# A matrix product with rotary embedding on one core: PSUM banks as separate tiles, half-width tiles in the last four pairs, and the first transposes inside the preceding tile

## The chip, the core and the metric

The kernel runs on one core of one Trainium2 chip. The metric is the device time of one execution in microseconds (us). Five engines with queues of their own work side by side: TensorE (PE in the profile) multiplies matrices and writes to PSUM, a memory of eight banks, each of which holds 512 fp32 columns on 128 partitions; VectorE (DVE), ScalarE (ACT) and GpSimd (POOL) do elementwise work; SyncE (SP) issues transfers. Any of SP, ACT and POOL can issue DMA transfers from its queue.

## The reference

```python
batch, seq, hidden, n_heads = (16, 512, 768, 12)      # head_dim = 64
y = np.matmul(x, weight)                              # (16, 512, 768) @ (768, 768), fp32
y = y.reshape(batch, seq, n_heads, head_dim)
y1, y2 = y[..., :32], y[..., 32:]                     # halves of every head
out1 = y1 * cos1 - y2 * sin1                          # cos, sin: (512, 64), cut the same way
out2 = y2 * cos2 + y1 * sin2
out = np.concatenate([out1, out2], axis=-1).reshape(batch, seq, hidden)
```

All of `x` (25 MB) is read and all of `out` (25 MB) is written once.

## The kernel before

**Tiles and pairs.** The 8192 rows of `x` are cut into 64 tiles of 128 rows. Two tiles form a pair; `n` from 0 to 31 counts the pairs (`NP` is 32), `s` is 0 or 1 within a pair, and this text numbers the tiles `i = 2n + s`. A pair's rows share their positions in the sequence, so one set of cos and sin values serves both of its tiles.

**The way of a tile.** SP loads it as fp32 (`xs`, ten buffers). ACT converts it to fp16 (`cast`, recorded at line 74). TensorE transposes it in six 128x128 pieces into a PSUM tile `pt` (`transpose`, line 124, two buffers), and ACT copies that back to SBUF as `xT` (line 74 again). Then TensorE does twelve matmuls (`mm`, line 167): six chunks of the contraction, each over 768 columns that lie in two PSUM banks, so 512 and 256 columns or the reverse. The two tiles of a pair fill one PSUM tile of three banks, of which there are two (`py_pool`). VectorE multiplies each result by cos and by the signed sin at once (`rope`, line 181, with an output `tq` twice as wide), GpSimd adds the two products with the halves of each head exchanged (`add`, line 192, into `ov`), and ACT issues the transfer that stores `ov` (`store`, line 241).

**Block pairs.** Pairs 8, 11, 14, ... 29 (`BLOCKS`) take another way: GpSimd's queue loads them, converted to fp16 on the way (`load_blocks`), and VectorE transposes them (line 131). Neither ACT nor TensorE's transposes take part.

**The order.** The program's order is the order of every engine's queue (`manual_schedule`). `upto("turn", k)` emits transposes until tiles below `k` have them, and `upto("cast", k)` the same for conversions. In the main loop the call after tile `i` is `upto("turn", i + 3)` and `upto("cast", i + 5)`; `upto` adds to `k` an extra lead that grows by one every four tiles from `k = 35` to at most six, so late in the kernel transposes run up to six tiles further ahead. At the start the tiles 0 to 3 are handled by hand around the loading of the weights, and `warm` runs matmuls of zeros until data is there.

**The end.** From pair 28 on (`ALONE = 4`) each tile has two banks of its own. Every third of them takes the two `pt` buffers (named `psz`), since no transpose needs these any more. Each tile is then multiplied, added and stored by itself. The stores of pairs 25, 26 and 27 are emitted at the end of pair 27, on ACT's queue. The last tile (`rope_last`) multiplies its last 256 columns as usual and then does the 512 others on VectorE alone, in three instructions at lines 220 and 224, after which SP stores them.

Of the kernel before, what the change touches and what calls it, by code (L numbers as in the profile page):

```python
# [10 lines left out]
FP32 = mybir.dt.float32  # L11
FP16 = mybir.dt.float16
# [5 lines left out]
def kernel(  # L18
# [9 lines left out]
    nc = tc.nc  # L28
    P = nc.NUM_PARTITIONS

    B, S, H = x.shape
    NH = int(n_heads)
    D = H // NH
    HD = D // 2
    R = 32
    NQ = P // R
    NT = H // (2 * P)
    SB = S // P
    NP = B * SB // 2
    CHUNKS = [(t, e) for t in range(NT) for e in range(2)]  # L40
    AHEAD = 7
    AHEAD_B = 8
    ALONE = 4
# [11 lines left out]
    cold = konst.tile([P, 512], FP16)  # L55
    sin_sb = konst.tile([P, SB, D], FP32)
    csn = konst.tile([P, 2, SB, D], FP32)
    w_raw = konst.tile([P, NT, 2, H], FP32)
    w_sb = konst.tile([P, NT, 2, H], FP16)

    xpool = ctx.enter_context(tc.tile_pool(name="xpool", bufs=10))
    bpool = ctx.enter_context(tc.tile_pool(name="bpool", bufs=5))
    cpool = ctx.enter_context(tc.tile_pool(name="cpool", bufs=6))
    tpool = ctx.enter_context(tc.tile_pool(name="tpool", bufs=11))
    rpool = ctx.enter_context(tc.tile_pool(name="rpool", bufs=3))
    opool = ctx.enter_context(tc.tile_pool(name="opool", bufs=6))
    pt_pool = ctx.enter_context(tc.tile_pool(name="pt", bufs=2, space=bass.MemoryType.PSUM))
    py_pool = ctx.enter_context(tc.tile_pool(name="py", bufs=2, space=bass.MemoryType.PSUM))

    xss, xhs, x16, xTT, psys, tqs, ovs = {}, {}, {}, {}, {}, {}, {}  # L70

# [47 lines left out]

    def transpose(n, s, eng):  # L120
        xc = x16.pop((n, s)).rearrange("p (t m e) -> p t e m", t=NT, e=2)
        pt = pt_pool.tile([P, NT, 2, P], FP16, tag="pt", name="pt")
        for t, e in CHUNKS:
            nc.tensor.transpose(pt[:, t, e, :], xc[:, t, e, :], ident)  # L124
        xT = tpool.tile([P, NT, 2, P], FP16, tag="xT", name="xT")
        copy(eng, xT, pt)
        xTT[n, s] = xT
# [12 lines left out]


    def psum(n, s):
        if n < NP - ALONE:
            if n not in psys:
                psys[n] = py_pool.tile([P, 3, 512], FP32, tag="psy", name="psy")
            cut = 512 if s == 0 else 256
            return [
                (psys[n][:, s, ds(s * 256, cut)], 0, cut),
                (psys[n][:, s + 1, 0 : H - cut], cut, H),
            ]  # L150
        if (n, s) not in psys:
            if (2 * (n - NP + ALONE) + s) % 3 == 1:
                psys[n, s] = [
                    pt_pool.tile([P, 512], FP32, tag="pt", name="psz") for _ in (0, 1)
                ]
            else:
                ps = py_pool.tile([P, 3, 512], FP32, tag="psy", name="psy")
                psys[n, s] = [ps[:, 0], ps[:, 1]]
        lo, hi = psys[n, s]
        return [(lo, 0, 512), (hi[:, 0 : H - 512], 512, H)]  # L160

    def mm(n, s, t, e, c0=0, c1=H):
        for k, (ps, lo, hi) in enumerate(psum(n, s)):
            a, z = max(c0, lo), min(c1, hi)
            if a >= z:
                continue
            nc.tensor.matmul(  # L167
                ps[:, a - lo : z - lo],
                xTT[n, s][:, t, e, :],
                w_sb[:, t, e, a:z],  # L170
                start=((t, e) == CHUNKS[0] and n > 1),
                stop=((t, e) == CHUNKS[-1] and (n > 1 or s >= k)),
            )

    def rope(n, c0, c1, ps):
        r = n % SB
        nh = (c1 - c0) // D
        if n not in tqs:
            tqs[n] = rpool.tile([P, 2, 2 * H], FP32, tag="tq", name="tq")
            ovs[n] = opool.tile([P, 2 * H], FP32, tag="ov", name="ov")  # L180
        nc.vector.tensor_tensor(  # L181
            out=tqs[n][:, :, c0:c1].rearrange("p j (h d) -> p j h d", d=D),
            in0=ps.rearrange("p (h d) -> p h d", d=D)
            .unsqueeze(1).broadcast_to((P, 2, nh, D)),
            in1=csn[:, :, r, :].unsqueeze(2).broadcast_to((P, 2, nh, D)),
            op=MULT,
        )

    def add(n, c0, c1, eng):
        w = c1 - c0  # L190
        tq = tqs[n][:, :, ds(c0, w)]
        eng.tensor_tensor(  # L192
            out=ovs[n][:, ds(c0, w)].rearrange("p (h t d) -> p h t d", t=2, d=HD),
            in0=tq[:, 0].rearrange("p (h t d) -> p h t d", t=2, d=HD),
            in1=tq[:, 1].rearrange("p (h t d) -> p h t d", t=2, d=HD)[:, :, ::-1, :],
            op=ADD,
        )

    def rope_pair(n, step=2 * H):
        ps = psys[n].rearrange("p b n -> p (b n)")  # L200
        for c in range(0, 2 * H, step):
            rope(n, c, c + step, ps[:, ds(c, step)])
            add(n, c, c + step, nc.gpsimd)

    def rope_alone(n, s):
        for ps, lo, hi in psum(n, s):
            rope(n, s * H + lo, s * H + hi, ps)

    def rope_last(n, s):
        (ps, _, cut), (pz, _, _) = psum(n, s)
        c0, c1, c2 = s * H, s * H + cut, (s + 1) * H
        rope(n, c1, c2, pz)
        add(n, c1, c2, nc.gpsimd)
        nh = cut // D
        q = tqs[n][:, 1, c0:c1]
        ph = ps.rearrange("p (h d) -> p h d", d=D)
        for o, j in ((q.rearrange("p (h d) -> p h d", d=D), 1), (ph, 0)):
            nc.vector.tensor_tensor(  # L220
                out=o, in0=ph, op=MULT,
                in1=csn[:, j, n % SB, :].unsqueeze(1).broadcast_to((P, nh, D)),
            )
        nc.vector.tensor_tensor(  # L224
            out=ovs[n][:, c0:c1].rearrange("p (h t d) -> p h t d", t=2, d=HD),
            in0=ps.rearrange("p (h t d) -> p h t d", t=2, d=HD),
            in1=q.rearrange("p (h t d) -> p h t d", t=2, d=HD)[:, :, ::-1, :],
            op=ADD,
        )
        store(n, nc.sync, c0, c1)  # L230
        store(n, nc.scalar, c1, c2)

    def store(n, eng, c0=0, c1=2 * H):
        b, r = where(n, 0)
        dst = out.rearrange("b (p r) h -> r p b h", r=SB)[r, :, b : b + 2]
        src = ovs[n].rearrange("p (b h) -> p b h", b=2)
        if c1 - c0 < 2 * H:
            s = c0 // H
            dst = dst[:, s, c0 - s * H : c1 - s * H]
            src = src[:, s, c0 - s * H : c1 - s * H]  # L240
        eng.dma_start(out=dst, in_=src)


    WARM = 17
    opened = [0]

    def warm(k):
        for _ in range(k):
            n, b = divmod(opened[0] % 6, 3)
            psum(n, 0)  # L250
            nc.tensor.matmul(  # L251
                psys[n][:, b], cold[:, 0:P], cold, start=True, stop=opened[0] < WARM - 6
            )
            opened[0] += 1

# [22 lines left out]
        load_pair(n)  # L278

    done = {"cast": 4, "turn": 4}

    def upto(what, k):
        k += min(6, max(0, k - 31) // 4)
        while done[what] < min(k, 2 * NP):
            n, s = divmod(done[what], 2)
            done[what] += 1
            if what == "cast":
                if n not in BLOCKS:  # L290
                    cast(n, s, nc.scalar)
            elif n in BLOCKS:
                transpose_blocks(n, s)
            else:
                transpose(n, s, nc.scalar)
# [33 lines left out]
    load_blocks(BLOCKS[0], (0, 2))  # L329
    load_blocks(BLOCKS[0], (1, 3))  # L330
    rope_pair(0)
    upto("cast", 6)
    for c in CHUNKS[4:]:
        mm(1, 0, *c)
    for c in CHUNKS[:3]:
# [1 line left out]
    upto("turn", 5)  # L337
    for c in CHUNKS[3:]:
        mm(1, 1, *c)
    upto("cast", 7)  # L340
    upto("turn", 6)
    upto("cast", 8)
    rope_pair(1)

    for n in range(2, NP):
        load_pair(n + AHEAD - 2)
        for m, quarters in ((n + AHEAD_B, (0, 2)), (n + AHEAD_B - 1, (1, 3))):
            if m > BLOCKS[0]:
                load_blocks(m, quarters)
        for s in (0, 1):  # L350
            for c in CHUNKS:
                mm(n, s, *c)
            upto("turn", 2 * n + s + 3)
            upto("cast", 2 * n + s + 5)
            if n >= NP - ALONE:
                if (n, s) != (NP - 1, 1):
                    rope_alone(n, s)
                    add(n, s * H, (s + 1) * H, nc.gpsimd)
                    store(n, nc.scalar, s * H, (s + 1) * H)
        if n < NP - ALONE:  # L360
            if n >= 3:
                store(n - 3, nc.scalar)
            rope_pair(n, H if n >= NP - ALONE - 2 else 2 * H)
        if n == NP - ALONE - 1:
            for m in (n - 2, n - 1, n):
                store(m, nc.scalar)
    rope_last(NP - 1, 1)


# [1 line left out]
_INS = ['x', 'weight', 'cos', 'sin', 'n_heads']  # L371
# [31 lines left out]
```

## Time and profile before

| What | Value |
|---|---|
| median of 8 runs | 158.37 us (158.28 to 158.71) |
| the profiled execution: its own time | 158.32 us |
| its span, first to last instruction | 156.5 us |
| granted TensorE clock, mean | 0.992 |
| busy: PE, DVE, ACT, POOL | 148.4, 124.9, 74.5, 129.1 us |
| DMA | 49.99 MB, mean 319 GB/s |

A line of the timeline gives the start in us, the time from the first start to the last end of the merged instructions, the engine, the line of the kernel, the operation, output and inputs, and how many instructions were merged; brackets hold the idle time before and what ended it. `ACTq`, `SPq` and `POOLq` are the engines' instruction queues, where transfers are issued. A line of the groups gives the shape of an instruction, how often it ran, its busy time in us and the mean duration of one in ns. Matmul records overlap: a matmul's end in the record is modelled, and the distance between two starts is what it costs TensorE.

### The profile page before, as it was taken

Reading aid. Unit: us, or ns where it says so; the run is one execution under the profiler, and the core shown is the slowest. Engines: PE = TensorE matmul, PEld = TensorE weight load, DVE = VectorE, ACT = ScalarE, POOL = GpSimd, SP = SyncE. Lnnn points to the kernel's source line nnn. Section 1 sums busy time; section 2 is a strip of 40 time slices with the busy share of each in tenths; the row PEclk is TensorE's granted clock in tenths of the full one; section 3 lists DMA queues with packets and bytes.
Section 4 is the critical chain, followed back from the end, with each engine's and each line's share of the span. In section 5 each row is a group of like instructions: output and inputs, shape, how many; then the busy total and the mean of one; then the engine's idle time right before and its main releaser. Section 6 shows DMA issues by size and latency. Waiting matters only on the chain.

```text
span 156.5 us, 2722 instructions
## 1 busy us (share of the span) xinstructions
PE 148.4 (95%) x1074; PEld 93.5 (60%) x1074; DVE 124.9 (80%) x78; ACT 74.5 (48%) x93; POOL 129.1 (82%) x77
## 2 busy tenths in 40 slices
PE   6999999999999999999999999999999999999930
PEld 2465666666656656666666666766667666656610
DVE  0656967876698698879869798879697899799990
ACT  3250967766526454660755665674746656200000
POOL 1000599999899899899989989997998779999990
PEclk9999999999999999999999999999999999999996
DMA  4999999999999999999999999999995725499655
GB/s 152 361 412 394 403 365 342 340 403 358 365 362 378 311 397 385 276 402 365 274 383 327 326 302 411 306 379 360 290 372 54 298 104 201 173 392 400 246 203 201
DMA packets 25837, 49.99 MB, mean 319 GB/s; under 512 B 10208, under 2 KB 10720, under 8 KB 25824
## 3 DMA queue, kind: packets, MB, share of 16 engines
q10 hardware_dynamic: 8768, 24.91, 40.9%
q1 hardware_dynamic: 8352, 21.76, 38.0%
q0 software_dynamic: 8704, 3.15, 17.5%
q8 instruction: 8, 0.13, 0.3%
q14 instruction: 5, 0.04, 0.1%
HBM read 27.79 MB, written 25.17 MB: 338 GB/s over the span
## 4 chain that ended last, share of the span: by engine, by line
PE 91%; DVE 4%; POOL 1%; POOLq 0%; issue 0%; DVEq 0%
PE psy L167 75%; PE pt L124 10%; PE psy L251 4%; DVE tq L181 3%; PE psz L167 2%; POOL ov L192 1%; POOLq L398 0%; DVE xT L76 0%; DVE cold L258 0%; DVE w_sb L111 0%; POOLq L192 0%; DVEq L181 0%
## 5 line engine op out<-in xcount | busy, mean ns | idle before, releaser
L167 PE MATMUL psy<-w_sb,xT 128*128 128x256 f16 (+1 forms) x733 | 126.7, 326 | 0.4 <-DVE w_sb L111 0.2
L181 DVE TENSOR_TENSOR tq<-psy,csn 128x3072 f32<-128x3072 f32 (+3 forms) x40 | 102.8, 2591 | 19.7 <-PE psy L167 19.7
L192 POOL TENSOR_TENSOR ov<-tq 128x1536 f32<-128x1536 f32 (+2 forms) x38 | 110.4, 2922 | 7.0 <-DVE tq L181 6.7
L167 PEld LDWEIGHTS <-xT 128*128 128x128 f16 x769 | 73.2, 98 | 45.7 <-DVE xT L131 0.8
L74 ACT COPY xT<-pt 128x768 f16<-128x768 f16 x46 | 36.4, 799 | 52.0 <-PE pt L124 50.5
L74 ACT CAST xc<-xs 128x768 f16<-128x768 f32 x46 | 40.4, 903 | 8.0 <-DMA xs<-in_x_dram 7.9
L124 PEld LDWEIGHTS <-xc 128*128 128x128 f16 x288 | 20.2, 99 | 6.8 <-DVE xc L76 0.9
L124 PE MATMUL pt<-ident,xc 128*128 128x128 f16 x288 | 23.9, 222 | 0.0
L103 POOL DMA_DIRECT2D xh<-in_x_dram x32 | 18.8, 591 | 0.0
L328 POOL COPY mark<-xs 128x1 f32<-128x1 f32 x1 | 0.2, 183 | 16.0 <-DMA xs<-in_x_dram 16.0
L131 DVE STREAM_TRANSPOSE xT<-xh 128x384 f32<-128x384 f32 x16 | 10.6, 690 | 0.0
L251 PE MATMUL psy<-cold 128*128 128x512 f16 x17 | 6.9, 557 | 1.2 <-DVE cold L258 1.2
L167 PE MATMUL psz<-w_sb,xT 128*128 128x512 f16 (+1 forms) x36 | 6.3, 326 | 0.0
L111 DVE CAST w_sb<-w_raw 128x768 f16<-128x768 f32 (+2 forms) x7 | 3.4, 500 | 2.0 <-DMA w_raw<-in_weight_dram 2.0
L76 DVE CAST xc<-xs 128x768 f16<-128x768 f32 x2 | 1.9, 948 | 3.2 <-DMA xs<-in_x_dram 3.2
L181 DVE TENSOR_TENSOR tq<-psz,csn 128x512 f32<-128x512 f32 (+1 forms) x5 | 4.3, 897 | 0.1
L251 PEld LDWEIGHTS <-cold 128*128 128x128 f16 x17 | 2.0, 131 | 3.5 <-issue 2.2
L76 DVE COPY xT<-pt 128x768 f16<-128x768 f16 x2 | 1.1, 558 | 1.6 <-PE pt L124 1.6
L74 ACT ACT_TABLE_LOAD x1 | 1.3, 1283 | 0.7 <-PEq L384 0.7
L258 DVE MEMSET cold<- 128x256 uint32 x1 | 0.3, 272 | 0.9 <-PEq L384 0.9
L224 DVE TENSOR_TENSOR ov<-psz,tq 128x512 f32<-128x512 f32 x1 | 0.7, 692 | 0.0
L220 DVE TENSOR_TENSOR psz<-psz,csn 128x512 f32<-128x512 f32 x1 | 0.7, 690 | 0.0
(9 smaller groups left out, 2.0 us busy)
## 6 DMA issues: line engine op xcount, KB each, us to landing
out_dram<-ov ACTq DMA_DIRECT2D x28, 768.0 KB, 7.2
xs<-in_x_dram SPq DMA_DIRECT2D x48, 384.0 KB, 6.7
xh<-in_x_dram POOLq DMA_DIRECT2D x32, 96.0 KB, 8.1
out_dram<-ov ACTq DMA_DIRECT2D x7, 384.0 KB, 2.4
w_raw<-in_weight_dram SPq DMA_DIRECT2D x5, 384.0 KB, 7.1
w_raw<-in_weight_dram SPq DMA_DIRECT2D x1, 256.0 KB, 5.7
out_dram<-ov SPq DMA_DIRECT2D x1, 256.0 KB, 2.6
w_raw<-in_weight_dram SPq DMA_DIRECT2D x1, 128.0 KB, 5.5
```

The source lines that it names most:

```text
L74: eng.copy(out=o, in_=i_)
L76: eng.tensor_copy(out=o, in_=i_)
L103: nc.gpsimd.dma_start(out=dst[ts(q, R)], in_=src[r, q])
L111: nc.vector.tensor_copy(out=w_sb[:, t, e, c0:c1], in_=w_raw[:, t, e, c0:c1])
L124: nc.tensor.transpose(pt[:, t, e, :], xc[:, t, e, :], ident)
L131: nc.vector.transpose(out=xT.bitcast(FP32).rearrange("p t (j a) o -> p t j (a o)", j=NQ), in_=x16.pop((n, s)).bitcast(FP32).rearrange("p ( ...
L167: nc.tensor.matmul(ps[:, a - lo : z - lo], xTT[n, s][:, t, e, :], w_sb[:, t, e, a:z], start=((t, e) == CHUNKS[0] and n > 1), stop=((t, e) ...
L181: nc.vector.tensor_tensor(out=tqs[n][:, :, c0:c1].rearrange("p j (h d) -> p j h d", d=D), in0=ps.rearrange("p (h d) -> p h d", d=D) .unsqu ...
L192: eng.tensor_tensor(out=ovs[n][:, ds(c0, w)].rearrange("p (h t d) -> p h t d", t=2, d=HD), in0=tq[:, 0].rearrange("p (h t d) -> p h t d", ...
L220: nc.vector.tensor_tensor(out=o, in0=ph, op=MULT, in1=csn[:, j, n % SB, :].unsqueeze(1).broadcast_to((P, nh, D)),)
L224: nc.vector.tensor_tensor(out=ovs[n][:, c0:c1].rearrange("p (h t d) -> p h t d", t=2, d=HD), in0=ps.rearrange("p (h t d) -> p h t d", t=2, ...
L251: nc.tensor.matmul(psys[n][:, b], cold[:, 0:P], cold, start=True, stop=opened[0] < WARM - 6)
```

## The change

PSUM is taken as single banks: `py_pool` has six buffers of one bank in place of two of three, and the multiplication by cos and sin runs bank by bank (`rope_bank`), the first bank of a pair right after the pair's first tile. In the last four pairs a tile is two halves of 384 columns, each in a bank of its own; `mm` runs all six chunks for one half, then for the other, and each half is multiplied and added by itself. Only the last half of the last tile goes through `rope_last`. For pairs 2 and 3 each tile's matmuls are cut at a column (256, or 512 for tile 4), and the transposes of the tile two further on, with the next conversion, stand between the two parts; the conversions of tiles 5 to 10 are emitted later than before. The growing extra lead in `upto` is gone, and `tpool` has 8 buffers in place of 11. In the last four pairs `upto` stands ahead of the tile's matmuls.

```diff
-    tpool = ctx.enter_context(tc.tile_pool(name="tpool", bufs=11))
+    tpool = ctx.enter_context(tc.tile_pool(name="tpool", bufs=8))
-    py_pool = ctx.enter_context(tc.tile_pool(name="py", bufs=2, space=bass.MemoryType.PSUM))
+    py_pool = ctx.enter_context(tc.tile_pool(name="py", bufs=6, space=bass.MemoryType.PSUM))
...
     def psum(n, s):
...
+        key, banks = (n, 3) if n < NP - ALONE else ((n, s), 2)
+        if key not in psys:
+            psys[key] = [
+                py_pool.tile([P, 512], FP32, tag="psy", name="psy") for _ in range(banks)
             ]
+        ps = psys[key]
+        if banks == 2:
+            return [(ps[k][:, 0:HH], k * HH, (k + 1) * HH) for k in (0, 1)]
+        cut = 512 if s == 0 else 256
+        return [(ps[s][:, ds(s * 256, cut)], 0, cut), (ps[s + 1][:, 0 : H - cut], cut, H)]
...
+    def rope_bank(n, b):
+        rope(n, b * 512, (b + 1) * 512, psys[n][b])
+
+    def add_pair(n, step=2 * H):
         for c in range(0, 2 * H, step):
-            rope(n, c, c + step, ps[:, ds(c, step)])
             add(n, c, c + step, nc.gpsimd)
...
+    def rope_pair(n):
+        for b in range(3):
+            rope_bank(n, b)
+        add_pair(n)
...
-    def rope_last(n, s):
-        (ps, _, cut), (pz, _, _) = psum(n, s)
-        c0, c1, c2 = s * H, s * H + cut, (s + 1) * H
-        rope(n, c1, c2, pz)
-        add(n, c1, c2, nc.gpsimd)
-        nh = cut // D
+    def rope_last(n, ps, c0, c1):
+        nh = (c1 - c0) // D
...
-        k += min(6, max(0, k - 31) // 4)
         while done[what] < min(k, 2 * NP):
...
     rope_pair(0)
-    upto("cast", 6)
+    upto("cast", 5)
...
     upto("turn", 5)
     for c in CHUNKS[3:]:
         mm(1, 1, *c)
-    upto("cast", 7)
-    upto("turn", 6)
-    upto("cast", 8)
+    upto("cast", 6)
     rope_pair(1)
...
         for s in (0, 1):
-            for c in CHUNKS:
-                mm(n, s, *c)
-            upto("turn", 2 * n + s + 3)
-            upto("cast", 2 * n + s + 5)
-            if n >= NP - ALONE:
-                if (n, s) != (NP - 1, 1):
-                    rope_alone(n, s)
-                    add(n, s * H, (s + 1) * H, nc.gpsimd)
+            i = 2 * n + s
+            if n < 4:
+                cut = 512 if i == 4 else 256
+                for c0, c1 in ((0, cut), (cut, H)):
+                    for c in CHUNKS:
+                        mm(n, s, *c, c0, c1)
+                    if c0 == 0:
+                        upto("turn", i + 2)
+                        upto("cast", i + 3)
+            elif n < NP - ALONE:
+                for c in CHUNKS:
+                    mm(n, s, *c)
+            upto("turn", i + 3 if i > 6 else 0)
+            upto("cast", i + 5 if i > 6 else 0)
+            if n < NP - ALONE:
+                for b in ((0,), (1, 2))[s]:
+                    rope_bank(n, b)
+                continue
+            for ps, lo, hi in psum(n, s):
+                for c in CHUNKS:
+                    mm(n, s, *c, lo, hi)
+                c0, c1 = s * H + lo, s * H + hi
+                if (n, s, hi) == (NP - 1, 1, H):
+                    rope_last(n, ps, c0, c1)
+                    store(n, nc.sync, c0, c1)
+                    continue
+                rope(n, c0, c1, ps)
+                add(n, c0, c1, nc.gpsimd)
+                if (n, s) == (NP - 1, 1):
+                    store(n, nc.scalar, c0, c1)
+                elif hi == H:
                     store(n, nc.scalar, s * H, (s + 1) * H)
         if n < NP - ALONE:
             if n >= 3:
                 store(n - 3, nc.scalar)
-            rope_pair(n, H if n >= NP - ALONE - 2 else 2 * H)
+            add_pair(n, H if n >= NP - ALONE - 2 else 2 * H)
         if n == NP - ALONE - 1:
             for m in (n - 2, n - 1, n):
                 store(m, nc.scalar)
-    rope_last(NP - 1, 1)
```

More of the change, by code (lines that the diff above doesn't have):

```diff
@@ L37 @@
     NT = H // (2 * P)
+    HH = H // 2
     SB = S // P
@@ L121, in transpose @@
         xc = x16.pop((n, s)).rearrange("p (t m e) -> p t e m", t=NT, e=2)
-        pt = pt_pool.tile([P, NT, 2, P], FP16, tag="pt", name="pt")
+        bank = pt_pool.tile([P, 8, P], FP16, tag="pt", name="pt")
+        pt = bank[:, 0 : 2 * NT].rearrange("p (t e) m -> p t e m", e=2)
         for t, e in CHUNKS:
@@ L142, in psum @@
     def psum(n, s):
[L143 to L149, printed above, removed]
-            ]
[L151 to L160, printed above, removed]
+        key, banks = (n, 3) if n < NP - ALONE else ((n, s), 2)
+        if key not in psys:
+            psys[key] = [
+                py_pool.tile([P, 512], FP32, tag="psy", name="psy") for _ in range(banks)
+            ]
+        ps = psys[key]
[3 more added lines that the diff above has]
+        return [(ps[s][:, ds(s * 256, cut)], 0, cut), (ps[s + 1][:, 0 : H - cut], cut, H)]
     def mm(n, s, t, e, c0=0, c1=H):
@@ L197, in add @@
         )
-    def rope_pair(n, step=2 * H):
-        ps = psys[n].rearrange("p b n -> p (b n)")
+    def rope_bank(n, b):
+        rope(n, b * 512, (b + 1) * 512, psys[n][b])
+    def add_pair(n, step=2 * H):
         for c in range(0, 2 * H, step):
-            rope(n, c, c + step, ps[:, ds(c, step)])
             add(n, c, c + step, nc.gpsimd)
-    def rope_alone(n, s):
-        for ps, lo, hi in psum(n, s):
-            rope(n, s * H + lo, s * H + hi, ps)
-    def rope_last(n, s):
-        (ps, _, cut), (pz, _, _) = psum(n, s)
-        c0, c1, c2 = s * H, s * H + cut, (s + 1) * H
-        rope(n, c1, c2, pz)
-        add(n, c1, c2, nc.gpsimd)
-        nh = cut // D
+    def rope_pair(n):
[4 more added lines that the diff above has]
+        nh = (c1 - c0) // D
         q = tqs[n][:, 1, c0:c1]
@@ L229, in rope_last @@
         )
-        store(n, nc.sync, c0, c1)
-        store(n, nc.scalar, c1, c2)
     def store(n, eng, c0=0, c1=2 * H):
@@ L251, in warm @@
             nc.tensor.matmul(
-                psys[n][:, b], cold[:, 0:P], cold, start=True, stop=opened[0] < WARM - 6
+                psys[n][b], cold[:, 0:P], cold, start=True, stop=opened[0] < WARM - 6
             )
```

## The prediction

> **What bounds the kernel now.** I read the page first: busy time, then the chain that ended last.
>
> ```profile
> span 156.5 us, 2722 instructions
> PE 148.4 (95%) x1074; PEld 93.5 (60%) x1074; DVE 124.9 (80%) x78; ACT 74.5 (48%) x93; POOL 129.1 (82%) x77
> ...
> PE 91%; DVE 4%; POOL 1%; POOLq 0%; issue 0%; DVEq 0%
> ```
>
> The chain is TensorE for 91% of the span: whatever makes TensorE wait lengthens the kernel, and only what shortens its queue, its waits or the tail behind it can gain. In the chain's list a tile's twelve matmuls take 1.95 us and six transposes 0.34 us, 2.29 together, so 512 of a tile's columns cost 1.30 and 256 cost 0.65. Next, the timeline of the start:
>
> ```profile
> 15.35 1.91 ACT L74 CAST xc<-xs 128x768 f16<-128x768 f32 x2 [4.65 <-DMA xs<-in_x_dram]
> ...
> 17.16 0.80 ACT L74 COPY xT<-pt 128x768 f16<-128x768 f16 x1
> ...
> 17.84 0.50 PE L124 MATMUL pt<-ident,xc 128*128 128x128 f16 x6
> 17.85 0.90 ACT L74 CAST xc<-xs 128x768 f16<-128x768 f32 x1
> ...
> 18.52 2.11 PE L167 MATMUL psy<-w_sb,xT 128*128 128x512 f16 x12 [0.18 <-DVE tq L181]
> ...
> 20.47 0.50 PE L124 MATMUL pt<-ident,xc 128*128 128x128 f16 x6
> ...
> 21.00 0.80 ACT L74 COPY xT<-pt 128x768 f16<-128x768 f16 x1 [0.76 <-PE pt L124]
> ```
>
> Two things are to be seen. The transposes from 17.84 are through at 18.18, yet tile 4's matmuls start at 18.52, when the multiplication of all of pair 0 lets its banks go: 0.34 us lost, the largest gap after the start. And the way from a transpose to a usable `xT` is long: transposes through at 20.81, ACT's copy from 21.00 to 21.80. ACT's next instruction starts 0.70 after a copy's start and 0.80 after a conversion's (17.16, 17.85, 18.65); TensorE starts about 0.13 after its operand is written (the conversion that ends at 5.29 is followed by transposes at 5.43). From then on TensorE runs without a break: tile 9 starts at 29.94, tile 56 at 134.21. Last, the end:
>
> ```profile
> 128.77 7.02 POOL L192 TENSOR_TENSOR ov<-tq 128x1536 f32<-128x1536 f32 x3 [1.09 <-DVE tq L181]
> ...
> 133.87 0.50 PE L124 MATMUL pt<-ident,xc 128*128 128x128 f16 x6
> ...
> 134.21 2.11 PE L167 MATMUL psy<-w_sb,xT 128*128 128x512 f16 x12
> 134.41 0.80 ACT L74 COPY xT<-pt 128x768 f16<-128x768 f16 x1 [1.49 <-PE pt L124]
> 134.41 18.66 ACTq L241 DMA_DIRECT2D out_dram<-ov  x12
> 135.98 16.71 POOL L192 TENSOR_TENSOR ov<-tq 128x768 f32<-128x768 f32 x10 [0.19 <-DVE tq L181]
> ...
> 150.62 0.68 DVE L220 TENSOR_TENSOR tq<-psz,csn 128x512 f32<-128x512 f32 x1
> 151.21 0.69 DVE L220 TENSOR_TENSOR psz<-psz,csn 128x512 f32<-128x512 f32 x1
> 151.94 0.69 DVE L224 TENSOR_TENSOR ov<-psz,tq 128x512 f32<-128x512 f32 x1
> 152.66 0.35 SPq L241 DMA_DIRECT2D out_dram<-ov  x1
> ```
>
> ACT's last copy is at 134.41, and all that follows on its queue are stores. Pair 25's sum was ready at about 132.2 (first of the three from 128.77), but its store left only behind that copy: ACT's queue goes in order, stores included. GpSimd then takes 16.71 us for ten sums, and ACT's queue sits in stores that wait for them, with nothing behind them. The last matmuls end at 134.21 + 8 x 1.95 = 149.81; the last store leaves SP at 152.66.
>
> **The start, part by part.** Bank by bank, pair 0's first bank is free after one instruction of 1.22 us (the 128x1024 row) in place of one of 3.36, at about 16.3, and the 0.34 goes. But the later order puts ACT on TensorE's path. Tile 5's conversion now follows tile 4's copy. Tile 4's copy starts at 16.87 + 0.20 = 17.07 (its transposes end at 16.87) and ends at 17.87, tile 4's matmuls start at 18.00 (TensorE was free at 17.84: 0.16 lost). Its 512 columns last to 19.30, tile 5's transposes (converted by 18.67) to 19.63, the other 256 columns to 20.29. Tile 5's copy runs 19.83 to 20.63, so tile 5 starts at 20.76: 0.47 lost. Its first 256 columns end at 21.42; tile 6's conversion, behind the copy, runs 20.53 to 21.43, its transposes start at 21.56: 0.14 lost. With 512 columns behind the transposes (1.30) tiles 6 and 7 come in time. In tile 7 two sets are due: tile 8's transposes end at 26.48, its copy starts at 26.68, the conversion of tile 9 at 27.38, done 28.28, and TensorE, through at 27.78, can transpose tile 9 only at 28.41: 0.63 lost. Tile 9's matmuls start at 31.03 against 29.94. Sum: 0.16 + 0.47 + 0.14 + 0.63 - 0.34 = +1.1 us. Tile 6 is cut into one piece more per chunk, six matmuls, at 0.11 each for 256 columns: the columns are the same, nothing. From tile 9 on the order is the old one.
>
> **The middle.** Three multiplications of 1.22 for one of 3.35 are 0.30 per pair, for pairs 0 to 27 8.4 us more on VectorE. What hides it is VectorE's idle time, 19.7 us behind TensorE in the waits, and each bank's own release, earlier than before; uncovered it would cost those 8.4. I take nothing. ACT's stores of pairs up to 24 find their sums long done. Loads wait for the buffers of tiles converted long before.
>
> **The end.** Without the extra lead, the transposes of tiles 57 and 60 to 63 come later: four sets (4 x 0.34) move from before tile 55's end to behind it. TensorE's sum is the same, but ACT's conversions and copies for tiles 60 to 63 now stand behind stores. Count from X, the end of pair 27's matmuls (before: 133.87; after: 133.87 + 1.1 - 1.34 = 133.6). VectorE starts the second bank at X + 0.27, the third at X + 1.40. GpSimd's two sums of pair 27 (1.82, or 1.77 where they follow closely) run X + 1.53 to X + 5.13, the store of pair 27 leaves at X + 5.16 and holds the queue for 0.38, and only then comes the conversion of tile 60: X + 5.6 to X + 6.5. TensorE had transposes of tile 57, tiles 56 and 57, through at X + 0.34 + 3.90 = X + 4.24; the next thing in its queue is tile 60's transposes, at X + 6.63: 2.4 us lost, with tile 58's matmuls, ready long since, queued behind. By rows the wait is at least 1.6 (the second sum starts as soon as the third bank is multiplied, at X + 2.6) and at most 3.0 (the store's issue takes 1.0, the longest of this line, in place of its 0.38).
>
> Later conversions and copies just come in time: tile 61's (behind the store of tile 56, whose second half is added by X + 7.05) is done at X + 8.4 for X + 8.9; tile 62's at X + 11.0 for X + 11.2; tile 63's at X + 13.2 for X + 13.5. So the matmuls end at X + 6.63 + 4 x 0.335 + 6 x 1.95 = X + 19.7 = 153.3, against 149.81.
>
> **The tail** gets shorter. The first half of the last tile is multiplied by 0.2 after the last matmul; then VectorE's last three instructions are 384 wide. The 512-wide ones take 2.01 from first start to last end; at 1.05 ns per column (681 to 1217 ns from 512 to 1024 elements) 384 wide they take 1.61, between 2.01 (nothing saved) and 1.0 (half). They end at 153.3 + 0.25 + 1.61 = 155.2, SP's store leaves 2.5 later than 152.66. A last transfer of 192 KB in place of 256 and 128 may give 0.1. GpSimd has no arrears after TensorE's stall: the last half's sum ends 1.2 after the matmuls. So 158.32 + 2.5 - 0.1 = 160.7 us; the profiled run was 0.05 below the median.
>
> **A rule on the clock.** The trace shows the clock's price at the start: a 512-column matmul cost 0.43 us (4.45 for ten) and costs 0.216 from 7.4 us on. A gap of 2.4 us on warm hardware is not in this trace; the bounds are no effect and the start's 5.9 us at half speed, which would add 2.95. I take none, the nearest rows being the 0.34 gap, behind which the matmuls run at full speed. The Trainium skill (TensorE: Matmul & The Clock Gate, Part 1: The HAM clock gate) says that the clock is halved only after about 3.4 us of idleness, and for such a window; by that the gap falls short and adds nothing, and a gap of 3.4 would add an estimated 1.7.
>
> **Rivals.** (1) The end alone: conversions at the start turn out early enough, the 0.34 is gained and 1.1 not lost: 160.7 - 1.4 = 159.3. For it speaks only that starts on ACT could shift by tenths. (2) The start alone: a waiting store does not hold the conversion behind it. Then the matmuls end at X + 17.3 = 150.9, VectorE at 152.8, GpSimd (after X + 1.53 two sums and 15 halves of 0.94, between the rows of 0.74 for 256 columns and 1.83 for 768) at 152.9; 158.6. Against it: the store that waited behind a copy. (3) The clock falls in the gap: up to 163.6. (4) Faster: ACT's work is never late, because it runs when its input is there and not in queue order. Then TensorE gains 0.34, matmuls end at 149.5, GpSimd's last half at 151.5, and its store leaves 1.2 ahead of 152.72: 157.1. It decides if tile 5's copy is done by 20.2 and tile 60's conversion by X + 4.1; the rows put them at 20.63 and X + 6.5.
>
> **Chances.** My forecast 0.70 (160.0 to 161.4 with the bounds), (1) 0.08, (2) 0.09, (3) 0.06, (4) 0.05, the rest elsewhere. The range 158.5 to 161.6 leaves out (3) and (4). 0.2%, 0.3 us, is about what a measurement of this kernel can tell from no change: faster 0.06, from (4); same 0.08, from (2); slower 0.86.
>
> **What would show it.** Right: transposes ahead of tile 58 that wait over 2 us for ACT's conversion, this behind a store on ACTq that leaves when pair 27's sums end; gaps of some 0.5 ahead of tiles 5 and 9; VectorE's last three rows near 0.55; more idle time of TensorE, and 84 bank-wide rows on VectorE. Wrong: TensorE without a gap after X, tile 9 at or before 29.94, or a gap between pairs in the middle that waits for VectorE.

## The result, and the profile after

The changed kernel takes 160.67 us in the median of 11 runs (159.19 to 161.59) against 158.42 us of 32 runs of the kernel before: a ratio of 1.0116, 95% interval 1.0093 to 1.0139. Slower, as forecast. But the median hides two groups: five of the runs lie between 159.19 and 159.66 us with a mean granted clock of 0.992 to 1.0, six between 160.67 and 161.59 with 0.982 to 0.986. With seven later executions of the same kernel it is 7 short ones against 11 long ones, 159.38 and 161.19 us in the mean. (One more long execution, of 161.18 us, stands outside the eleven and is not counted.) The profiled execution, 159.57 us, is a short one. Its page:

```profile
span 157.4 us, 2813 instructions
PE 148.1 (94%) x1080; PEld 93.1 (59%) x1080; DVE 129.8 (82%) x132; ACT 75.2 (48%) x93; POOL 130.5 (83%) x84
PE 80%; DMA 6%; POOL 3%; DVE 2%; SPq 2%; ACT 2%; issue 2%; ACTq 0%
```

TensorE does the same 148 us of work; its share of the chain fell from 91% to 80%. ACT, which had no part in it, has 2% now, and GpSimd 3% in place of 1%. The transfers' 6% are not the change's: 4.6 of them are the load of the weights ahead of the first real matmuls, where this chain runs through the load and that of the kernel before through the matmuls of zeros, and 1.5 are the last store. Its timeline at the start:

```profile
20.66 0.83 PE L161 MATMUL psy<-w_sb,xT 128*128 128x256 f16 x6 [0.24 <-ACT xT L75]
...
28.25 0.51 PE L126 MATMUL pt<-ident,xc 128*128 128x128 f16 x6 [0.40 <-ACT xc L75]
...
30.89 2.11 PE L161 MATMUL psy<-w_sb,xT 128*128 128x256 f16 x12
```

Tile 5 waits for ACT's copy, the transposes of tile 9 for ACT's conversion, and tile 9 starts at 30.89 where it started at 29.94: 0.95 us lost. (The brackets give idle time by modelled ends; from the distances of the starts the two gaps are 0.40 and 0.56 us.) And at the end, with the same columns:

```profile
133.93 4.68 ACTq L231 DMA_DIRECT2D out_dram<-ov  x4
134.60 7.42 POOL L186 TENSOR_TENSOR ov<-tq 128x768 f32<-128x768 f32 x6 [0.31 <-POOL ov L186]
...
138.64 0.90 ACT L75 CAST xc<-xs 128x768 f16<-128x768 f32 x1 [4.00 <-POOL ov L186]
...
139.59 0.51 PE L126 MATMUL pt<-ident,xc 128*128 128x128 f16 x6 [1.94 <-ACT xc L75]
139.94 2.11 PE L161 MATMUL psy<-w_sb,xT 128*128 128x384 f16 x12
...
152.85 0.56 DVE L212 TENSOR_TENSOR tq<-psy,csn 128x384 f32<-128x384 f32 x1
153.32 0.56 DVE L212 TENSOR_TENSOR psy<-psy,csn 128x384 f32<-128x384 f32 x1
153.91 0.56 DVE L216 TENSOR_TENSOR ov<-psy,tq 128x384 f32<-128x384 f32 x1
154.50 0.35 SPq L231 DMA_DIRECT2D out_dram<-ov  x1
```

The four stores that begin at 133.93 end at 138.61, the last of them once GpSimd has both sums of pair 27; ACT's conversion of tile 60 starts 0.03 behind, and TensorE, through with tile 57 at 137.49, transposes tile 60 at 139.59: a gap of 2.10 us. The last store leaves at 154.50, 1.84 later than before, but lands sooner (1.9 us for its 192 KB, where 256 KB took 2.6), so the span is only 0.9 longer. That is the short group. What makes the long one is the subject of the first experiments.

### The profile page after: what moved, and what is told of

The parts are those of the page before. It is cut to its first block, busy times and chain, and to the rows that moved or that the text cites. A ratio compares the mean times of both kernels' runs of the same rounds, so it can differ in the third digit from the quotient of the medians.

```text
span 157.4 us, 2813 instructions
## 1 busy us (share of the span) xinstructions
PE 148.1 (94%) x1080; PEld 93.1 (59%) x1080; DVE 129.8 (82%) x132; ACT 75.2 (48%) x93; POOL 130.5 (83%) x84
## 4 chain that ended last, share of the span: by engine, by line
PE 80%; DMA 6%; POOL 3%; DVE 2%; SPq 2%; ACT 2%; issue 2%; ACTq 0%
PE psy L161 71%; PE pt L126 9%; DMA w_raw<-in_weight_dram 5%; POOL ov L186 3%; DMA out_dram<-ov 1%; DVE tq L175 1%; ACT xc L75 1%; SPq L109 1%; SPq L82 1%; ACT xT L75 1%; DVE w_sb L112 0%; DVE ov L216 0%; DVE psy L212 0%; ACTq L231 0%
## 5 line engine op out<-in xcount | busy, mean ns | idle before, releaser
L161 PE MATMUL psy<-w_sb,xT 128*128 128x256 f16 (+2 forms) x775 | 133.0, 324 | 0.8 <-DVE w_sb L112 0.5
L175 DVE TENSOR_TENSOR tq<-psy,csn 128x1024 f32<-128x1024 f32 (+1 forms) x99 | 112.5, 1173 | 17.0 <-PE psy L161 15.8
L186 POOL TENSOR_TENSOR ov<-tq 128x1536 f32<-128x1536 f32 (+2 forms) x45 | 111.8, 2498 | 6.8 <-DVE tq L175 4.1
L161 PEld LDWEIGHTS <-xT 128*128 128x128 f16 x775 | 73.8, 98 | 45.3 <-ACT xT L75 0.8
L126 PEld LDWEIGHTS <-xc 128*128 128x128 f16 x288 | 19.5, 98 | 10.5 <-ACT xc L75 4.1
L133 DVE STREAM_TRANSPOSE xT<-xh 128x384 f32<-128x384 f32 x16 | 11.2, 701 | 0.0
L241 PE MATMUL psy<-cold 128*128 128x512 f16 x17 | 6.0, 495 | 1.2 <-DVE cold L248 1.2
L216 DVE TENSOR_TENSOR ov<-psy,tq 128x384 f32<-128x384 f32 x1 | 0.6, 558 | 0.0
L212 DVE TENSOR_TENSOR tq<-psy,csn 128x384 f32<-128x384 f32 x1 | 0.6, 557 | 0.0
L212 DVE TENSOR_TENSOR psy<-psy,csn 128x384 f32<-128x384 f32 x1 | 0.6, 555 | 0.0
```

The lines of the kernel that those rows point to most:

```text
L133: nc.vector.transpose(out=xT.bitcast(FP32).rearrange("p t (j a) o -> p t j (a o)", j=NQ), in_=x16.pop((n, s)).bitcast(FP32).rearrange("p ( ...
L161: nc.tensor.matmul(ps[:, a - lo : z - lo], xTT[n, s][:, t, e, :], w_sb[:, t, e, a:z], start=((t, e) == CHUNKS[0] and n > 1), stop=((t, e) ...
L175: nc.vector.tensor_tensor(out=tqs[n][:, :, c0:c1].rearrange("p j (h d) -> p j h d", d=D), in0=ps.rearrange("p (h d) -> p h d", d=D) .unsqu ...
L186: eng.tensor_tensor(out=ovs[n][:, ds(c0, w)].rearrange("p (h t d) -> p h t d", t=2, d=HD), in0=tq[:, 0].rearrange("p (h t d) -> p h t d", ...
L241: nc.tensor.matmul(psys[n][b], cold[:, 0:P], cold, start=True, stop=opened[0] < WARM - 6)
```

## The experiments

Theory: TensorE's wait for ACT costs twice, by the gap and by a clock that falls in it. The rivals: the two groups come from transfers or the tail; the gap has another cause than ACT's queue; GpSimd has no part in the end.

**The same kernel again.**

> The changed kernel once more, unchanged. Its eleven times lie in two groups, 159.2 to 159.7 and 160.7 to 161.6 us, with granted clocks of 0.992 to 1.0 and of 0.982 to 0.986. Theory (the clock falls in TensorE's wait of 2.1 us ahead of tile 58 in about half of the executions): the groups come again, some 1.6 us apart, none between, the longer one with a clock lower by 0.01, which at half speed is about 3.3 us and so 1.6 us lost. If the profiled execution falls into the longer group, the matmuls of 384 columns behind the gap cost 0.32 us for about 3 us and 0.16 later; in the shorter group 0.16 at once. Rival (the groups come from transfers or from the tail): the lower clock lies behind the last matmul only, and the gap and the matmuls behind it are the same in both.

> The changed kernel unchanged, one profiled execution, to see one of the longer group if it falls there (161.2 us): the clock theory expects half speed for about 3.4 us directly behind the 2.1 us gap, the matmuls of 384 columns 0.32 us apart, and the same gaps as in the shorter ones. In a shorter one (159.3): 0.16 at once.

Measured: 159.20 and 159.22 with clocks 0.992 and 0.996, and 161.09 to 161.31 with 0.982 to 0.985, nothing between. The single later execution, 161.28 us at a clock of 0.985, is a long one, and profiled. Its gap is the same 2.10 us, ending at 139.71. The timeline of TensorE behind the gap, then busy time and clock by stretches (columns: stretch, us, busy time of PE, PEld, DVE, ACT, POOL, the granted clock, the busy share of the DMA engines and GB/s):

```profile
139.71 0.51 PE L126 MATMUL pt<-ident,xc 128*128 128x128 f16 x6 [1.94 <-ACT xc L75]
140.05 3.46 PE L161 MATMUL psy<-w_sb,xT 128*128 128x384 f16 x12
143.31 0.85 PE L126 MATMUL pt<-ident,xc 128*128 128x128 f16 x6
143.95 2.18 PE L161 MATMUL psy<-w_sb,xT 128*128 128x384 f16 x12
```

```profile
137.24:140.64 3.40, 1.46 (x14) 0.84 (x12) 3.10 (x4) 0.89 (x1) 3.40 (x4) 1.00 1.01 386
140.66:144.06 3.40, 3.40 (x17) 1.97 (x15) 1.47 (x2) 2.33 (x3) 2.47 (x3) 0.50 1.02 397
144.08:147.40 3.32, 3.32 (x26) 2.12 (x25) 2.34 (x3) 1.48 (x3) 2.18 (x3) 1.00 0.57 227
```

The first tile behind the gap takes 3.46 us in the record where the short execution's takes 2.11. The granted clock is 0.50 from 140.66 to 144.06 and full on both sides: 3.4 us at half speed, 1.7 lost, which is the distance of the groups. The matmuls end at 154.43 against 152.65 in the short one. The rival on transfers falls.

**The gap filled.**

```diff
+            if i == 58:
+                fill = py_pool.tile([P, 512], FP32, tag="psy", name="fill")
+                for _ in range(9):
+                    nc.tensor.matmul(fill, cold[:, 0:P], cold, start=True, stop=True)
             upto("turn", i + 3 if i > 6 else 0)
```

> Nine matmuls of zeros, 512 columns each, into a bank of their own, stand ahead of the transposes that wait for tile 60's conversion: they fill 1.94 us of the 2.1 us gap and change nothing else. Theory (the clock falls because TensorE idles): one group only, 159.2 to 159.8 us, median 159.5, clock 0.99 or more. Rival (the groups have another cause): two groups as before, median between 159.5 and 161.

Measured: 159.42 us, 159.18 to 160.02, clocks 0.992 to 1.0 in all six: the long group is gone. TensorE in the place of the gap:

```profile
137.73 2.11 PE L353 MATMUL fill<-cold 128*128 128x512 f16 x9
139.85 0.51 PE L126 MATMUL pt<-ident,xc 128*128 128x128 f16 x6
```

The transposes of tile 60 come as late as before, but of the wait only 0.18 us are idle (nine matmuls at 0.216 from 137.73 on last to 139.67). Idleness lowers the clock, not the wait as such.

**The gap lengthened** by one and by two idle copies on ACT:

```diff
+            if i == 56:
+                for _ in range(2):          # 1 in the shorter version
+                    nc.scalar.copy(out=junk, in_=w_raw[:, 0, 0, :])
             upto("cast", i + 5 if i > 6 else 0)
```

> Two more copies of 0.8 us on ScalarE's queue (into a tile that nothing reads) ahead of tile 60's conversion: TensorE's gap grows from 2.1 to about 3.7 us. Clock theory: nearly all executions fall into the longer group, 159.5 + 1.6 + 1.6 = 162.7 us, clock about 0.983. By the Trainium skill (TensorE: Matmul & The Clock Gate, Part 1: The HAM clock gate) a window of 3.4 us of idleness is what halves the clock, so a gap of 3.7 would do it always and one of 2.1 never. Rival (another cause): two groups again, near 161.1 and 162.7.

> One more copy of 0.8 us ahead of tile 60's conversion: a gap of 2.9 us, between the 2.1 of the changed kernel, where 10 of 17 executions were longer by 1.7 us, and the 3.7 where all six were. If the clock is judged by windows of a fixed length that start at any time, a longer gap meets it more often: at least four of six executions near 160.1 + 1.7 = 161.8, the others near 160.1. If there were a threshold between 2.1 and 2.9, all six near 161.8.

Measured: gaps of 3.69 and 2.84 us. With the long one all six executions lie between 162.41 and 163.60, median 162.68, as forecast; the profiled one again shows a clock of half for 3.4 us. With the middle one three lie at 160.00 to 160.30 and three at 161.57 to 162.25: fewer long ones than the four I had asked for, but a mixture, so no sharp length of the gap decides between 2.1 and 2.9. The last section says what does.

**The lead put back.**

```diff
+        k += min(6, max(0, k - 31) // 4)
         while done[what] < min(k, 2 * NP):
```

(and 11 buffers in `tpool`.)

> The changed kernel with the growing extra lead of transposes and conversions put back (and 11 buffers for it): the conversions of tiles 60 to 63 stand ahead of the stores of pairs 25 to 27. If the gap is the store's work: no gap of TensorE behind pair 27, one group of times, clock 0.99 or more. The time does not fall by the 2.1 us of the gap, since GpSimd becomes the last: its sums from 134.6 + 1.34 on are two of 1.77 and fifteen of 0.965, to 154.0, against 154.50 for the last store now; so 159.0 us. Rival (GpSimd has slack to spare there): 159.5 - 2.1 = 157.4. If the gap has another cause, it stays and so do both groups.

Measured: 159.42 us, 159.13 to 159.53, one group. No gap behind pair 27; the matmuls end at 150.62, 2.03 earlier than in the short execution of the changed kernel. And yet the time is that of the short group, since GpSimd is last. Its timeline:

```profile
147.25 6.71 POOL L186 TENSOR_TENSOR ov<-tq 128x384 f32<-128x384 f32 x7
149.23 5.10 ACTq L231 DMA_DIRECT2D out_dram<-ov  x4
...
151.88 0.56 DVE L216 TENSOR_TENSOR ov<-psy,tq 128x384 f32<-128x384 f32 x1
152.47 0.35 SPq L231 DMA_DIRECT2D out_dram<-ov  x1
```

VectorE is through at 152.44, GpSimd, without a pause, only at 153.97 (147.25 + 6.71 in the merged row), 154.0 being forecast. The lead wins the gap and loses it again: it takes the transposes of four tiles from behind pair 27 to before it, so pair 28, and GpSimd's last stretch with it, starts later, and that stretch is now the longest. In the changed kernel GpSimd is nearly as late (its last sum ends at 153.94, the last store leaves at 154.50).

**Stores moved from ACT to SP**, those of pairs 25 to 27 alone, then all from pair 25 on but the last tile's first half:

```diff
             for m in (n - 2, n - 1, n):
-                store(m, nc.scalar)
+                store(m, nc.sync)
```

```diff
                 elif hi == H:
-                    store(n, nc.scalar, s * H, (s + 1) * H)
+                    store(n, nc.sync, s * H, (s + 1) * H)
```

> The changed kernel with the stores of pairs 25, 26 and 27 issued by SP instead of ACT; the stores of the tiles behind them stay on ACT. If ACT's queue order is the cause, the gap moves by one tile: tile 60's conversion runs early, tile 61's now stands behind the store of tile 56 (ACT, 6.9 us after pair 27's matmuls) and is done at about X + 8.2, where X is the end of pair 27's matmuls, while TensorE is there at X + 6.5: a gap of about 1.8 us ahead of tile 61's transposes, 0.3 more ahead of tile 62's, none ahead of tile 60's. The matmuls end at X + 19.4 as now: shorter executions 159.3, and others longer by 1.6 where the clock falls. Rival (the first store alone is at fault): no gap at all, 158.0.

> The changed kernel with all stores from pair 25 on issued by SP, but for the last two. Nothing on ACT's queue waits for GpSimd any more: no gap behind pair 27, one group of times. Matmuls end at X + 17.3 = 150.5, VectorE's last instruction at 152.4, GpSimd's last sum at 134.6 + 2 x 1.77 + 15 x 0.965 = 152.6, against 154.0 in the kernel with the lead put back, where the matmuls of pair 28 start 1.3 later: 158.0 us. If the lead were needed for anything but ACT's order, this would be slower than that kernel's 159.42.

Measured with the three alone: 159.67 us. Its timeline, TensorE and ACT:

```profile
137.46 0.50 PE L126 MATMUL pt<-ident,xc 128*128 128x128 f16 x6
...
141.53 0.51 PE L126 MATMUL pt<-ident,xc 128*128 128x128 f16 x6 [1.61 <-ACT xc L75]
```

```profile
140.13 0.35 ACTq L231 DMA_DIRECT2D out_dram<-ov  x1
140.58 0.89 ACT L75 CAST xc<-xs 128x768 f16<-128x768 f32 x1 [5.16 <-POOL ov L186]
```

Tile 60's transposes follow at once (137.46) and the gap stands one tile further on, ahead of tile 61's, behind the store at 140.13: 1.78 us, and 0.60 more ahead of tile 62's (0.3 forecast). It is the order of ACT's queue, whichever store stands there. No execution was long, though the expectation allowed for some: clocks of 0.994 to 1.0 in all six. With all the stores on SP: 158.14 us (ratio to the kernel before 0.9974, 0.9961 to 0.9988). GpSimd's sums and tile 60's transposes in its timeline:

```profile
134.47 18.01 POOL L186 TENSOR_TENSOR ov<-tq 128x768 f32<-128x768 f32 x17 [0.28 <-POOL ov L186]
...
137.37 0.50 PE L126 MATMUL pt<-ident,xc 128*128 128x128 f16 x6
```

There is no gap ahead of tile 60's transposes or later, and GpSimd's last sum ends at 152.48 (134.47 + 18.01), 1.49 ahead of the kernel with the lead. The time is 1.2 us under the mean of the short group: that is what the gap costs apart from the clock, in the same order of TensorE's work. The lead is not needed for itself; without it the matmuls of pair 28 start 1.5 earlier (133.47 against 150.62 - 8 x 1.95 = 135.02), and GpSimd with them.

**The start put back**, on top of the lead: the order of the kernel before for the tiles up to 8.

```diff
-    upto("cast", 5)
+    upto("cast", 6)
...
-    upto("cast", 6)
+    upto("cast", 7)
+    upto("turn", 6)
+    upto("cast", 8)
...
-            if n < 4:
...
-            elif n < NP - ALONE:
+            if n < NP - ALONE:
```

> The lead put back, and the start of the kernel before put back too (no transposes inside a tile, conversions of tiles 5 to 8 early); single banks and halves stay. Against the kernel with the lead alone (159.42): the gaps ahead of tiles 5, 6 and 9 (0.40, 0.14, 0.56) are gone, 1.1, and the transposes of tile 5 come at 17.84 with the first bank free by then, so tile 4 starts at 18.2 where it started at 18.52 before: about 1.3 less in all, 158.1 us, GpSimd still last. If the start's transposes inside a tile were no loss, 159.4.

Measured: 158.18 us against 159.42, 1.24 less; the gaps ahead of tiles 4, 5, 6 and 9 are gone, and with them the 0.34 of the kernel before. Single banks, halves and the shorter end on VectorE alone are thus worth 0.9979 (0.9968 to 0.9991) of the kernel before: little, since GpSimd ends at 152.75, no earlier than before (152.69).

**Whole sums at the end**, on top of that:

```diff
-                add(n, c0, c1, nc.gpsimd)
                 if (n, s) == (NP - 1, 1):
+                    add(n, c0, c1, nc.gpsimd)
                     store(n, nc.scalar, c0, c1)
                 elif hi == H:
+                    add(n, s * H, (s + 1) * H, nc.gpsimd)
```

> As the kernel with lead and start put back, and in the last four pairs GpSimd adds a whole tile of 768 columns at once (but for the last tile's first half); VectorE still multiplies by halves. Seven tiles cost 1.774 each on GpSimd in place of 2 x 0.965: 1.1 less behind the matmuls. GpSimd's last sum then ends at 151.6, VectorE's last instruction at 151.2: 157.0 us. If GpSimd did not set the end: no change from the kernel without this edit, 158.1.

Measured: 157.42 us (0.993, 0.9916 to 0.9944). GpSimd's last sum ends at 151.53, 1.22 sooner; the medians differ by 0.76. Of the 1.22, 0.25 is not the edit's: in the profiled execution the matmuls, which the edit does not touch, already end 0.25 sooner (149.13 against 149.38). Counted from the end of the matmuls GpSimd gains 0.97, for 1.1 expected. The other 0.2 lies within the spread of the executions (157.04 to 157.55, and 157.82 to 158.55 without the edit).

**All of it**: stores on SP, no lead, the old start, whole sums.

> What the runs so far say is good, together: single banks, halves in the last four pairs, no extra lead, the stores from pair 25 on issued by SP, the start of the kernel before, and whole sums of 768 columns at the end. Against the kernel with the stores on SP (158.14): 1.3 less by the start, and GpSimd's last sum 1.1 less behind the matmuls, so that VectorE's last three instructions are the last: matmuls end at 150.40 - 1.27 = 149.13, VectorE at 151.0, the last store leaves 1.5 ahead of the 152.51 there: 156.6 us, 0.8 under the best so far (157.42). If the lead in the transposes had a worth of its own, no better than 157.4.

Measured: 156.72 us (0.9895, 0.9879 to 0.9911), 0.1 from what was expected and 1% under the kernel before. The end of its timeline:

```profile
150.46 0.56 DVE L216 TENSOR_TENSOR ov<-psy,tq 128x384 f32<-128x384 f32 x1
151.33 0.35 ACTq L231 DMA_DIRECT2D out_dram<-ov  x1
```

VectorE ends at 151.02 (150.46 + 0.56) and the last store leaves at 151.33, where the kernel before has 152.63 and 152.72; the matmuls end at 149.19. One thing was expected otherwise: GpSimd, not VectorE, is still the last, by 0.27. Its last sum ends at 151.29, and the store at 151.33 is the one that waits for it.

## Why the prediction was right, and where it was not

**ACT's queue.** Right in mechanism and place: the gap stands ahead of tile 58's matmuls, ends with the conversion behind pair 27's store, moves on by a tile when the stores of pairs 25 to 27 leave ACT's queue, and goes when the later ones leave it too. Its size was 2.10 for 2.4: GpSimd's first sum of pair 27 began 1.35 after the matmuls, not 1.53 (134.60 against 133.25), the conversion 5.39 after, not 5.6, and TensorE started 0.05 behind it, not 0.13.

**The start.** Right: four gaps of 0.08, 0.40, 0.14 and 0.56 for 0.16, 0.47, 0.14 and 0.63, and tile 9 0.95 late for 1.1. Three of them were put some 0.07 too large, by the 0.13 that I took from the first transposes, at half clock, for TensorE's restart: behind ACT's copy, at 20.66, it is 0.05.

**The middle.** Taken at nothing, it gained 0.19: the kernel before has three waits of 0.06 (at 45.3, 58.4 and 71.5 us) that the changed one does not have. Its table of waits names them:

```profile
PEld L167 <- DVE xT L131: 0.8, 3, 0.3
```

(0.8 us in total, three times, 0.3 the longest, on the engine's weight loads; the distance of two matmuls grows by 0.06.) TensorE waits there for a block pair's `xT`, which VectorE transposes only behind a multiplication of 3.36 us. In the changed kernel the multiplications are bank-wide, and the transposes come in between. So the gain comes from the order of VectorE's queue, not from the earlier release of PSUM banks. VectorE's 4.9 us more of busy time (129.8 against 124.9; 8.4 had been reckoned) were hidden.

**The tail.** VectorE ends 1.83 after the matmuls, 1.86 forecast, and its three rows take 0.56. The last transfer was mis-sized: from issue to landing it gave 0.7 (1.9 for 2.6), not 0.1. The runs do not show why: it is smaller, but so was the kernel before's other last store, 128 KB in 2.7.

**The clock.** This step failed: "by that the gap falls short and adds nothing". It adds 1.7 to 1.8 us in 11 of 18 executions: half speed for 3.4 us behind a gap of 2.1, which the prediction had held too short for it. The 1.7 that it estimated for a gap of 3.4 is what this one cost. Rival (3) had the mechanism, at too high a price (2.95) and too small a chance.

**The sum.** Without the clock it should have read 160.7 - 0.1 (start) - 0.2 (middle) - 0.3 (gap) - 0.6 (transfer) = 159.5, where the short group lies (159.57 in the profiled execution); with it 161.2, the long group. That the median is the 160.7 of the forecast is luck: terms too large by 1.2 met a term of 1.7 that was left out and comes in more than half of the executions, and 160.67, the sixth of the eleven times, is the shortest of the long group (over all 18 the median is 161.1). The direction rests on the mechanism; the fit of the number does not.

**What the sum did not show.** I let TensorE's gap carry the end and said that GpSimd had no arrears behind it. It had few, because of the gap: without it GpSimd, with halved sums at 0.96 each where half of a whole one takes 0.89, is the last, and of the 2.1 only 1.2 is won with the stores on SP, and nothing with the lead. These arrears are in rival (2), whose 158.6 the kernel with the stores on SP stands for: 158.14. Rival (4), faster, supposed an ACT without queue order; the same end is reached by taking the waiting stores off ACT's queue, with the old start and whole sums: 156.72.

## What to carry to other kernels

Look at what stands behind a store in an engine's queue: a store waits for its data, and everything that the program puts behind it waits too, so an engine that feeds the bottleneck should not issue the stores of the slowest one, or should have its feeding done before. Smaller pieces shorten the work behind the last matmul, but may cost more in sum: here VectorE's halves shortened the tail, and GpSimd's halves (0.96 each for 1.77 whole) took it back, as GpSimd was the last. When the times of a kernel lie in two groups, compare the granted clock of the runs before averaging: one wait of TensorE can be the cause of both.

## What the hardware showed

The granted clock goes by windows of 3.41 us, which lie elsewhere in each execution. In the three profiled drops half speed begins at 140.65 (gap of 2.10 us), 140.57 (2.84) and 140.85 (3.69), lasts 3.41 us, and the next drop, behind the last matmul, comes another 13.65 us later, four times 3.41. Counted back by 40 windows of 3.413 from 140.65 one comes to 4.12, and there the first matmuls of zeros go from 0.43 to 0.22 us apart. The gap does not set the beginning: half speed starts 0.94 us behind the end of the gap of 2.10, 0.15 ahead of that of 2.84 and 0.27 ahead of that of 3.69.

What decides is how long TensorE idles within one window. The windows below are counted in steps of 3.41 us from a change of the clock in the same trace; the idle time is the part of the gap, or of the time behind the last matmul, that lies in the window.

| Execution | Window, us | Idle in it, us | Clock in the next |
|---|---|---|---|
| changed kernel, 159.22 us: gap | 137.52 to 140.94 | 1.72 | 1.00 |
| all of it: behind the last matmul | 147.53 to 150.95 | 1.76 | 1.00 |
| changed kernel, 159.57 us: gap | 137.68 to 141.09 | 1.91 | 1.00 |
| the same: behind the last matmul | 151.33 to 154.75 | 2.10 | 1.00 |
| changed kernel, 161.28 us: gap | 137.24 to 140.65 | 2.10 | 0.50 |
| gap of 3.69: behind the last matmul | 154.51 to 157.92 | 2.23 | 0.50 |
| changed kernel, 159.22 us: behind the last matmul | 151.18 to 154.59 | 2.29 | 0.50 |
| gap of 2.84: gap | 137.16 to 140.57 | 2.69 | 0.50 |
| gap of 3.69: gap | 137.44 to 140.85 | 3.41 | 0.50 |

So the limit in these traces is about 2.1 us of idleness in 3.41. Since the windows lie elsewhere in each execution, a gap of 2.10 halves the clock only when it falls whole into one. An estimate from this: a gap of length g has 2.1 us in one window in a share (3.41 + g - 4.2) / 3.41 of its positions, 0.38 for 2.10, 0.60 for 2.84 and 0.85 for 3.69; seen were 11 of 18, 3 of 6 and 6 of 6. The 1.78 us with 0.60 more, 2.29 later, never have 2.1 in one window, and none of 6 was long.

The Trainium skill (TensorE: Matmul & The Clock Gate, Part 1: The HAM clock gate) states that the clock is halved after an idle window of about 3.4 us, in windows that run freely. The length and the free running are what these traces show; the idleness needed is not: 2.1 us of the 3.41 were enough.
